# Five buffers in place of three for the samples' raw key pages, in a decoder step on one core

## The chip, the cores and the metric

The kernel runs on one core of one Trainium2 chip. The metric is the device time of one execution in microseconds (us), lower is better. A core has a matrix engine (TensorE, PE in the rows; PEld is its weight load), a vector engine (VectorE, DVE), a scalar engine (ScalarE, ACT), a general engine (GpSimd, POOL) and a queue that issues transfers (SyncE, SP); a q behind an engine's name (SPq, ACTq) is its sequencer. Transfers run on 16 DMA engines.

## The reference, cut to what matters

One step of a two-layer decoder trunk: a gated short convolution, then sparse attention with three branches (compressed, selected, window) that share one set of keys and values. There are 512 prompt tokens and 8 samples of one token each; a sample has 2048 past rows in 16 pages of 128 rows. The part that matters here is the attention of the samples:

```python
def nsa_sample(q, gate, cmp_tok, new_sel, win_all, page_table, pool_sel):
    ...
    def one(q_b, g_b, cmp_b, new_b, win_b, pages):
        def fetch(kp):
            in_past = kp < past_len
            page = pages[jnp.clip(kp // PAGE_SIZE, 0, n_pages - 1)]
            old = pool_sel[page, kp % PAGE_SIZE, :, hidx, :]
            ...
        return nsa_attend(q_b, g_b, pos, cmp_b, fetch, n_blocks, win_b, win_pos)
```

In nsa_attend the scores over the compressed keys give an importance of each block of 64 keys; the 16 most important blocks are attended to, and so are the window's last 512 keys. The kernel does not gather: it scores all 16 pages of every sample and masks the blocks that were not chosen.

## The kernel before, in words

Everything is float32, and the large products are done as three matmuls on split operands (mm3, lines 114 to 116). After the convolution and the query projections the stage that matters begins, at about 740 us of the profiled span. Two streams are written into one another there by mix (line 228):

- The main stream, kvz_steps: the products for the keys and values of the prompt (kv_work, four of them) and for the gate z (z_work, four). It has 68 steps: nine for each kv_work (eight of four matmul triples, and one for the samples' own rows), eight for each z_work (four triples each). Their weights come through a single buffer (wraw, loaded at line 384 from the ACT queue), and are split on ACT and DVE (lines 103, 104).
- The side stream, sample_steps: the samples' attention. RK = 0.8 steps of it are taken for each main step, 54 in all.

The side stream's first part is sample_keys (line 1146). It loads the compressed keys in two halves (kc, line 1191), scores them (line 1180), and works out which blocks are chosen; for that it loads a constant table (lt, line 1215) that DVE reads at line 1221. Then come 40 tiles of raw keys, here called page tiles 1 to 40. Each holds 4 pages (128 rows by 256 numbers each, 512 KB in a tile). Tiles 1 to 32 hold the selected branch's pages and cost SP two register loads of page numbers (line 1356) and four transfers (line 1361); tiles 33 to 40 hold window rows and cost two transfers (line 1370). A page tile is turned by eight transposes on PE (line 1245), copied from PSUM by ACT and DVE into a kt tile (lines 1251, 1249), and each second tile is followed by 16 matmuls for the scores (line 1180). Page tile p belongs to side step 4 + p (for the first 32), so the code's order puts it beside main step (4 + p) / 0.8, rounded up.

kc's two halves, lt, and the 40 page tiles all come from raw_t, in this order, 43 requests in all. raw_t gives a tile of the ring skv, which has three buffers of 4 KB a partition; while the pool pr does not exist (it is made in attention, line 939, after the stage), this is its only source. A new load waits until PE has done the transposes of the tile that had the buffer.

The second part is sample_values (line 1285): softmaxed scores S are transposed into PT (lines 1301 to 1306), a tile of 22 blocks of 128 columns, 11 KB a partition, and the value pages are multiplied by it (line 1320). PT is allocated there, as the last tile of the pool `at`; values are loaded through raw_v, which takes two of three from the kt ring and the third from raw_t.

On SP the stage's instructions keep the order in which the code writes them; on the other engines the order is fixed ahead, by a planner that simulates the program and takes what it believes to be ready. An engine executes its list in order. When the main stream is through, attention loads its constants and the prompt's keys (KK, lines 931 and 1011) into room that the main stream's tiles had, and its first scores are line 1053.

Of the kernel before, what the change touches and what calls it, by code (L numbers as in the profile page):

```python
# [8 lines left out]
F32 = mybir.dt.float32  # L9
# [64 lines left out]
def dram(ap, offset, dims):  # L74
    return bass.AP(tensor=ap.tensor, offset=ap.offset + offset, ap=dims)


class Yoco:
# [10 lines left out]
    at_prompt = None  # L89
    n_raw = 0  # L90
    n_val = 0
    at_w = {}
    pr = None

# [1033 lines left out]
    def sample_setup(self):  # L1128
        self.cst = {}
        self.load_consts(self.at, ("grp", "mem", "mb", "em", "sel"))  # L1130
        self.S = self.at.tile([128, 2704], F32, name="S")

    def raw_t(self):
        self.n_raw += 1
        if self.pr and self.n_raw % (3 + SK) >= 3:
            return self.pr.tile([128, 4, 256], F32, name="skv2", bufs=SK)
        return self.at.tile([128, 4, 256], F32, name="skv", bufs=3)

    def raw_v(self):

        self.n_val += 1
        if self.n_val % 3 == 0:
            return self.raw_t()
        return self.at.tile([128, 2, 512], F32, name="kt", bufs=4).rearrange("p a (b n) -> p (a b) n", b=2)

    def sample_keys(self):

        nc = self.nc
        at = self.at
        I = self.I  # L1150
        cst = self.cst
        S = self.S
        raw_t = self.raw_t
        QF = at.tile([128, 2, 128], F32, name="QF")
        QZ = at.tile([128, 2, NS, 32], F32, name="QZ")
        sm = at.tile([128, 16], F32, name="sm")
# [5 lines left out]
        for kvh in range(4):  # L1162
            hp, h2 = divmod(kvh, 2)
            a = slice(h2 * 64, h2 * 64 + 64)
# [24 lines left out]
        for par in range(2):  # L1189
            kc = raw_t()  # L1190
            nc.sync.dma_start(kc, dram(self.KCd, par * 128 * 256, [[256, 128], [2 * 128 * 256, 4], [1, 256]]))
            scores(acc[:, :128], par, lambda j, hp: kc[:, j, hp * 128:hp * 128 + 128], par == 0, par == 1)
            yield
# [18 lines left out]
        sc = S[:, 256:286]  # L1212
        nc.vector.tensor_copy(sc, ps[:, :30])
        lt = raw_t().rearrange("p a n -> p (a n)")[:, :900].rearrange("p (a n) -> p a n", a=30)
        nc.sync.dma_start(lt, dram(I["consts"], self.lt_at, [[NCONST, 128], [30, 30], [1, 30]]))
        c1 = S[:, 512:1412].rearrange("p (a n) -> p a n", a=30)
# [13 lines left out]
        for br in range(2):  # L1230
            base = 2056 * br
            for c in range(4 if br == 0 else 1):
                d = S[:, base + c * 512:base + (c + 1) * 512]
                acc = self.ps.tile([128, 512], F32, name="acc1", bufs=1)
                for par in range(2):
                    for half in range(2):
                        kt = []
                        for i in range(2):
                            raw = raw_t()
                            pair = at.tile([128, 2, 512], F32, name="kt", bufs=4)  # L1240
                            self.load_keys(raw, br, (4 * i + par, 4 * i + 2 + par), c * 4 + half * 2)
                            for hp in range(2):
                                ps = self.psum1()
                                for x in range(4):
                                    nc.tensor.transpose(ps[:, x * 128:(x + 1) * 128],  # L1245
                                                        raw[:, x, hp * 128:(hp + 1) * 128], self.ident)
                                k = pair[:, hp]
                                if hp:
                                    nc.vector.tensor_copy(k, ps)
                                else:  # L1250
                                    nc.scalar.activation(k, ps, AF.Copy)
                                kt.append(k)
                            if i:
                                scores(acc[:, half * 256:half * 256 + 256], par,
                                       lambda j, hp: kt[j // 2 * 2 + hp][:, j % 2 * 256:j % 2 * 256 + 256],
                                       par == 0 and half == 0, par == 1 and half == 1)
                            yield
# [27 lines left out]
    def sample_values(self):  # L1285

        nc = self.nc
        at = self.at
        cst = self.cst
        S = self.S  # L1290
        raw_t = self.raw_t
        OS = at.tile([128, KT, NS], F32, name="OS")
        PT = at.tile([128, 22, 128], F32, name="PT")
        nc.gpsimd.memset(PT[:, 21], 0.0)

        at_ = [t * 128 for t in range(16)] + [2056 + t * 128 for t in range(4)] + [2576]
        for t in range(0, 21, 4):
            n = min(4, 21 - t)
            ps = self.psum1()
            for i in range(n):  # L1300
                nc.tensor.transpose(ps[:, i * 128:(i + 1) * 128], S[:, at_[t + i]:at_[t + i] + 128], self.ident)
            d = PT[:, t:t + n].rearrange("p t x -> p (t x)")
            if t % 8:
                nc.vector.tensor_copy(d, ps[:, :n * 128])
            else:
                nc.scalar.activation(d, ps[:, :n * 128], AF.Copy)
            yield
        for br in range(2):
            ps = self.psum1()
            a = 2048 + br * 520  # L1310
            nc.tensor.transpose(ps[:NS, :128], S[:, a:a + NS], self.ident)
            nc.vector.tensor_copy(PT[br * 32:br * 32 + NS, 21], ps[:NS, :128])
        yield
        acc = self.ps.tile([128, 512], F32, name="acc1", bufs=1)
        for par in range(2):
            def values(t, rhs, first=None, behind=None):
                for j in (3, 0, 1, 2):
                    q = first or behind
                    with self.tc.issue_after(q.ins) if q else ExitStack():
                        m = nc.tensor.matmul(acc[j * 32:j * 32 + 32, par * 256:par * 256 + 256],  # L1320
                                             PT[:, t, j * 32:j * 32 + 32], rhs(j),
                                             start=par == 0 and t == 20, stop=par == 1 and t == 18)
                    first = first or m
                return first

            vc = raw_t()
            nc.sync.dma_start(vc, dram(self.VCd, par * 128 * 256, [[256, 128], [2 * 128 * 256, 4], [1, 256]]))
            values(20, lambda j: vc[:, j])
            values(21, lambda j: self.VN)
            yield  # L1330

            for t in range(0, 20, 2):
                raw = [self.raw_v(), self.raw_v()]
                for i in range(2):
                    self.load_values(raw[i], t // 16, par, t % 16 + i)

                first = None
                for i in (1, 0):
                    first = values(t + i, lambda j: raw[i][:, j], first, self.at_prompt)
                yield  # L1340
        om = S[:, 0:512]
        nc.vector.tensor_tensor(om, acc, cst["em"], op=ALU.mult)
        nc.vector.tensor_tensor(om[:, 0:256], om[:, 0:256], om[:, 256:512], op=ALU.add)
        ps = self.ps.tile([128, 512], F32, name="acc1", bufs=1)
        for hp in range(2):
            nc.tensor.matmul(ps[:, hp * 32:hp * 32 + 32], om[:, hp * 128:(hp + 1) * 128], cst["sel"],
                             start=True, stop=True)
        nc.vector.tensor_copy(OS.rearrange("p k b -> p (k b)"), ps[:, :64])
        nc.vector.tensor_tensor(OS, OS, self.SZ[:, :, NT:], op=ALU.mult)
        self.split(self.OZS[:, :, 0:NS], self.OZS[:, :, 32:40], OS)  # L1350
        yield
# [165 lines left out]
```

## Time and profile before

| | us |
|---|---|
| runs shown | 1180.73, 1181.22, 1184.16 |
| median | 1181.22 |
| the profiled execution's own time | 1182.27 |
| span of its instructions | 1180.4 |
| PE busy in the span | 1127.1 (95%) |
| DVE, ACT, POOL busy | 686.2, 583.1, 276.1 |

All times of the rows are counted from the span's start. The profiled execution is 1.05 us above the median of the runs, and 1.9 us of it lies outside the span. A stage's limit is read from the idle time of PE inside it and from what ended that idle time.

### The profile page before, as it was taken

What the parts mean: (1) busy time and instruction counts of PE and PEld (TensorE: products, weight loads), DVE (VectorE), ACT (ScalarE), POOL (GpSimd) and SP (SyncE); (2) the same over time, 40 slices, a digit from 0 to 9 for tenths busy, and PEclk for the clock granted to TensorE, in tenths of its full rate; (3) what the DMA queues carried; (4) which work ended last, traced back from release to release, by engine and by line L of the source; (5) the groups of instructions that cost most, each with busy time, mean ns of one, the idle gap of its engine ahead of it and who ended that gap; (6) DMA issues with size and microseconds to landing.
All of it is one profiled execution on the core that took longest, in us unless ns stands there. A gap on an engine that the chain in (4) does not pass through costs nothing.

```text
span 1180.4 us, 23314 instructions
## 1 busy us (share of the span) xinstructions
PE 1127.1 (95%) x8882; PEld 1030.6 (87%) x8882; DVE 686.2 (58%) x1532; ACT 583.1 (49%) x1183; POOL 276.1 (23%) x382
## 2 busy tenths in 40 slices
PE   6999999999999999999999999998999898999896
PEld 4999999999999999999999999877888765766796
DVE  4865464455644555554557466542454698898952
ACT  5454343353343443434446465342445677787651
POOL 5221200201101111012002101120110464565631
PEclk9999999999999999999999999998999899999998
DMA  7564754564446645357532542587986557576011
GB/s 208 154 221 135 252 177 116 188 199 153 135 122 204 199 134 161 119 141 236 162 112 56 134 99 80 157 263 215 244 229 182 204 183 222 170 221 281 2 57 71
DMA packets 161072, 194.81 MB, mean 165 GB/s; under 512 B 48096, under 2 KB 139720, under 8 KB 160312
## 3 DMA queue, kind: packets, MB, share of 16 engines
q1 hardware_dynamic: 122928, 125.32, 35.9%
q0 software_dynamic: 12832, 46.20, 11.6%
q10 hardware_dynamic: 25200, 21.79, 6.4%
q8 instruction: 70, 1.15, 0.4%
q14 instruction: 42, 0.34, 0.1%
HBM read 168.96 MB, written 32.75 MB: 171 GB/s over the span
## 4 chain that ended last, share of the span: by engine, by line
PE 66%; DMA 9%; DVE 9%; issue 8%; ACT 3%; SPq 3%; POOL 3%; POOLq 0%; ACTq 0%; DVEq 0%
PE mm L115 13%; PE mm L116 13%; PE mm L114 13%; PE tr L618 3%; PE acc L116 2%; PE acc L114 2%; PE s L1053 2%; PE acc L115 2%; DMA wrawx<-in_conv_w_in 2%; PE tr L1245 1%; PE acc L1320 1%; PE acc L1115 1%; DVE pp L1060 1%; DMA skv<-in_cache_sel_kv 1%; PE acc L1116 1%
## 5 line engine op out<-in xcount | busy, mean ns | idle before, releaser
L114 PE MATMUL mm<-X,wh 128*128 128x260 f32 (+1 forms) x1008 | 290.3, 288 | 3.2 <-ACT X L355 1.4
L115 PE MATMUL mm<-X,wl 128*128 128x260 f32 (+1 forms) x1008 | 286.1, 284 | 0.1
L116 PE MATMUL mm<-X,wh 128*128 128x260 f32 (+1 forms) x1008 | 285.6, 284 | 0.5 <-DVE X L360 0.5
L114 PEld LDWEIGHTS mm<-X,wh 128*128 128x128 f32 (+1 forms) x1008 | 188.7, 187 | 6.1 <-ACT X L355 1.7
L115 PEld LDWEIGHTS mm<-X,wl 128*128 128x128 f32 (+1 forms) x1008 | 188.8, 187 | 3.5 <-DVE wl L104 0.3
L116 PEld LDWEIGHTS mm<-X,wh 128*128 128x128 f32 (+1 forms) x1008 | 188.6, 187 | 3.7 <-DVE X L360 0.7
L606 POOL DMA_INDIRECT G<-in_cache_cmp_kv,cidx x64 | 62.9, 982 | 329.5 <-ACT Gp L612 163.6
L100 ACT ACTIVATE th<-tr 128x512 fp32r<-128x512 f32 x128 | 71.8, 594 | 96.9 <-PE tr L618 96.5
L101 DVE TENSOR_TENSOR tl<-tr,th 128x512 fp32r<-128x512 f32 x128 | 84.5, 683 | 50.7 <-ACT th L100 50.7
L114 PE MATMUL mm<-X,whx 128*128 128x260 f32 x288 | 81.6, 283 | 0.7 <-ACT whx L100 0.7
L1078 POOL TENSOR_SCALAR pp<-pp,pst,gt 128x128 f32<-128x128 f32 (+3 forms) x128 | 76.6, 612 | 23.9 <-DVE pst L1075 14.9
L115 PE MATMUL mm<-X,wlx 128*128 128x260 f32 x288 | 82.0, 285 | 0.0
L116 PE MATMUL mm<-X,whx 128*128 128x260 f32 x288 | 81.7, 284 | 0.0
L1063 ACT ACTIVATE pp<-pp,pst 128x128 f32<-128x128 f32 (+3 forms) x128 | 70.8, 555 | 13.6 <-DVE pst L1060 12.7
L101 DVE TENSOR_TENSOR wl<-wraw,wh 128x1024 fp32r<-128x1024 f32 x38 | 49.5, 1307 | 40.7 <-ACT wh L100 40.5
L618 PE MATMUL tr<-ident,Gp 128*128 128x128 f32 x512 | 70.7, 272 | 1.2 <-DVE Gp L614 1.2
L100 ACT ACTIVATE wh<-wraw 128x1024 fp32r<-128x1024 f32 x38 | 39.9, 1056 | 54.0 <-PE mm L116 41.0
L618 PEld LDWEIGHTS tr<-ident,Gp 128*128 128x128 f32 x512 | 59.3, 140 | 4.1 <-DVE Gp L614 1.4
L1060 DVE CUSTOM_DVE_ANT_0 pp<-s,c_mw 128x128 f32<-128x128 f32 (+3 forms) x128 | 57.9, 481 | 3.1 <-PE tx L1103 2.2
L114 PEld LDWEIGHTS mm<-X,whx 128*128 128x128 f32 x288 | 54.3, 188 | 2.3 <-ACT whx L100 0.9
L115 PEld LDWEIGHTS mm<-X,wlx 128*128 128x128 f32 x288 | 54.2, 188 | 2.1
L116 PEld LDWEIGHTS mm<-X,whx 128*128 128x128 f32 x288 | 54.4, 189 | 1.3
(434 smaller groups left out, 2849.4 us busy)
## 6 DMA issues: line engine op xcount, KB each, us to landing
skv<-in_cache_sel_kv SPq DMA_DIRECT2D x172, 128.0 KB
wraw<-in_conv_w_in SPq DMA_DIRECT2D x16, 1024.0 KB
wrawx<-in_conv_w_in SPq DMA_DIRECT2D x16, 1024.0 KB
kt<-in_cache_sel_kv SPq DMA_DIRECT2D x84, 128.0 KB
wo<-wo_scratch SPq DMA_DIRECT2D x4, 2048.0 KB
out_win_kv_s<-in_cache_win_kv ACTq DMA_DIRECT2D x8, 1022.0 KB
wrawx<-in_conv_w_out SPq DMA_DIRECT2D x4, 1024.0 KB
wraw<-in_conv_w_out SPq DMA_DIRECT2D x4, 1024.0 KB
```

Of the source, the lines that this page charges most:

```text
L100: nc.scalar.activation(hi, src, AF.Copy)
L101: nc.vector.tensor_tensor(lo, src, hi.bitcast(F32), op=ALU.subtract)
L114: mm(out, sh, mh, start=first, stop=False)
L115: mm(out, sl, mh, start=False, stop=False)
L116: mm(out, sh, ml, start=False, stop=last)
L606: nc.gpsimd.indirect_dma_start(out=G.rearrange("p i c d -> p (i c d)"), out_offset=None, in_=table, in_offset=bass.IndirectOffsetOnAxis(ap ...
L618: nc.tensor.transpose(ps[:, h * 128:(h + 1) * 128], Gp[:, c * 4 + h, :], self.ident)
L1053: nc.tensor.matmul(out, QK[:, g], KK[:, s, cs], start=s == 0, stop=s == 1)
L1060: nc.vector.tensor_tensor_reduce(out=d, in0=src, in1=m, scale=-SCALE, scalar=1e28, op0=ALU.add, op1=ALU.min, accum_out=mx[:, g, i:i + 1])
L1063: nc.scalar.activation(d, d, AF.Exp, scale=-1.0, bias=mx[:, g, i:i + 1], accum_out=l[:, g, i:i + 1])
L1078: nc.gpsimd.tensor_scalar(P[g2][:, i, :W], P[g2][:, i, :W], f[:, g2, i + 1:i + 2], gates[:, g2, i + 1:i + 2], op0=ALU.mult, op1=ALU.mult)
L1115: nc.tensor.matmul(acc, v, ph, start=i == 0, stop=False)
```

## The change: a place of five for the key pages

PT is allocated in sample_setup, behind S, and so lives for the whole stage. sample_keys takes its raw tiles from raw_k in place of raw_t: of each five requests three go to the ring skv as before, and two to fixed places in PT (blocks 0 to 7 and 8 to 15, 4 KB a partition each). sample_values takes the same PT.

```diff
@@ class Yoco
     n_raw = 0
     n_val = 0
+    n_key = 0
@@ sample_setup
         self.S = self.at.tile([128, 2704], F32, name="S")
+        self.PT = self.at.tile([128, 22, 128], F32, name="PT")
@@
+    def raw_k(self):
+
+        self.n_key += 1
+        i = self.n_key % 5
+        if i < 3:
+            return self.raw_t()
+        return self.PT[:, (i - 3) * 8:(i - 2) * 8].rearrange("p t x -> p (t x)").rearrange("p (a n) -> p a n", n=256)
+
@@ sample_keys
-        raw_t = self.raw_t
+        raw_t = self.raw_k
@@ sample_values
-        PT = at.tile([128, 22, 128], F32, name="PT")
+        PT = self.PT
         nc.gpsimd.memset(PT[:, 21], 0.0)
```

Request 1 and 2 (kc) go to the ring, 3 (lt) to PT's first place, 4 (page tile 1) to its second, 5, 6 and 7 (page tiles 2 to 4) to the ring, 8 (page tile 5) to PT's first place, 9 to its second, and so on.

## Rows read from the trace of the kernel before

**Rows 1.** Busy time by stretch (us, each engine's busy time with count, clock, DMA share, GB/s).

```profile
740.00:922.00 182.00, 173.69 (x1574) 152.53 (x1572) 80.78 (x172) 76.81 (x149) 19.47 (x27) 0.98 0.71 206
780.00:800.00 20.00, 15.92 (x147) 12.60 (x149) 8.11 (x15) 7.60 (x15) 6.06 (x7) 1.00 0.84 271
```

**Rows 2.** PE in order of time (start, length), where page tiles 9 to 12 begin.

```profile
787.68 0.51 PE L1245 MATMUL tr<-ident,skv 128*128 128x128 f32 x2 [1.39 <-DMA skv<-in_cache_sel_kv]
...
792.12 0.67 PE L1245 MATMUL tr<-ident,skv 128*128 128x128 f32 x2 [0.28 <-DMA skv<-in_cache_sel_kv]
...
799.11 0.33 PE L1245 MATMUL tr<-ident,skv 128*128 128x128 f32 x1 [2.40 <-DMA skv<-in_cache_sel_kv]
...
802.74 0.48 PE L1245 MATMUL acc<-ident,skv 128*128 128x128 f32 x1 [1.10 <-DMA skv<-in_cache_sel_kv]
```

**Rows 3.** Busy time by stretch, the two stretches around them at the lower clock.

```profile
800.48:807.31 6.83, 5.73 (x27) 5.33 (x28) 1.76 (x4) 2.19 (x5) 0.00 (x0) 0.50 0.74 249
926.78:937.02 10.24, 9.71 (x47) 8.53 (x47) 6.57 (x55) 6.64 (x28) 3.64 (x9) 0.50 1.04 388
```

**Rows 4.** SP's own waits, 744 to 915 us (us in total, times, longest).

```profile
SPq L1361 <- PE tr L1245: 7.8, 4, 3.7
...
SPq L1361 <- PE acc L1180: 3.1, 1, 3.1
...
SPq L1361 <- PE acc L1245: 2.3, 2, 1.8
```

**Rows 5.** Line 1361 from 745 to 883 us (ns min/median/max, first and last start).

```profile
L1361 SPq DMA_DIRECT2D skv<-in_cache_sel_kv x128: 332/333/1178, 749.1 to 881.6; - x128
```

**Rows 6.** SP in order of time: kc, then the first transfer of page tiles 1, 5, 9.

```profile
733.20 0.93 SPq L1191 DMA_DIRECT2D skv<-kc_scratch  x2
...
749.12 0.37 SPq L1361 DMA_DIRECT2D skv<-in_cache_sel_kv  x1
...
764.96 0.33 SPq L1361 DMA_DIRECT2D skv<-in_cache_sel_kv  x1
...
782.50 0.33 SPq L1361 DMA_DIRECT2D skv<-in_cache_sel_kv  x1
```

**Rows 7.** DVE in order of time: the read of lt.

```profile
760.78 1.09 DVE L1221 TENSOR_TENSOR S<-S,skv 128x900 f32<-128x900 f32 x1
```

**Rows 8.** PE in order of time, the end of the main stream and attention's start.

```profile
921.43 0.28 PE L115 MATMUL mm<-X,wl 128*128 128x260 f32 x1
921.55 0.28 PE L116 MATMUL mm<-X,wh 128*128 128x260 f32 x1
...
924.02 0.64 PE L1320 MATMUL acc<-skv,PT 128*32 128x256 f32 x8 [2.08 <-DVE PT L1304]
924.75 0.66 PE L1301 MATMUL tr<-ident,S 128*128 128x128 f32 x4
...
927.33 1.08 PE L1320 MATMUL acc<-VN,PT 128*32 128x256 f32 x8
928.93 6.04 PE L1053 MATMUL s<-KK,QA 128*128 128x160 f32 x24 [0.53 <-DMA KK<-kk_scratch]
```

**Rows 9.** POOL in order of time, the same stretch.

```profile
921.90 0.98 POOL L943 MEMSET pb<- 128x512 f32 x2 [53.61 <-PE mm L116]
922.83 0.73 POOL L1011 DMA_DIRECT2D KK<-kk_scratch  x1
```

**Rows 10.** Line 1301 (ns min/median/max, first and last start, forms).

```profile
L1301 PE MATMUL tr<-ident,S x16: 270/273/330, 916.4 to 925.1; 128*128 128x128 f32 x16
```

**Rows 11.** Line 1282, the same columns.

```profile
L1282 DVE TENSOR_SCALAR S<-S,sm x2: 482/882/1283, 899.5 to 924.2; 128x2056 f32<-128x2056 f32 x1, 128x520 f32<-128x520 f32 x1
```

**Rows 12.** Line 114 by stretch: the main stream's matmuls before page tiles 11 and 32.

```profile
739.60:796.16 56.56, 23.44 (x81) 15.19 (x81) 1.00 0.66 207
739.60:887.08 147.48, 61.00 (x206) 39.49 (x206) 0.98 0.77 222
```

**Rows 13.** The chain of work that ended last, one piece (start, us).

```profile
764.66 7.17 DMA wraw<-in_w_kv
```

## The prediction

> **What bounds the kernel now.** I read the table of times first, then PE's busy time by stretch, then PE in order of time wherever it idles, then SP's own waits, and the end of the stage last. In the stage that the change touches, 740 to 922 us, PE is busy 173.7 of 182 us [rows 1]: PE is the bound, and all that this stage can give is its 8.3 us of idle time and whatever PE runs at half clock. The worst piece is 780 to 800 us, with 4.1 us idle. PE in order of time shows where: four times PE starts the transposes of a page tile and stands until the rest of it has landed, 1.39, 0.28, 2.40 and 1.10 us, released by the transfer of page tiles 9 to 12 [rows 2]. That is 5.17 us. Right behind it the granted clock is 0.50, so 1.2 of 2.4 GHz, from 800.48 to 807.31 us [rows 3]; PE stood until 802.74 [rows 2], so 4.57 us of work ran at half speed, which at full speed takes half: 2.3 us. Stalls and clock make 7.5 us, 0.6% of the run.
>
> Is the ring of three what makes the pages late? Only in part. From 745 to 883 us SP issues 128 page transfers for 32 tiles in 132.5 us, 4.14 us a tile [rows 5], and its waits for PE, which are the waits for a free buffer, add up to 13.2 us [rows 4]: 3.1 for kc's scores and 10.1 for transposes. Without them a tile costs (132.5 - 13.2) / 32 = 3.7 us of SP's own issuing, which no buffer removes. So the ring costs SP a tenth of its pace, and its own issuing nine tenths.
>
> **The change part by part.** *Page tile 1* moves from a kc buffer to PT's second place, which nothing holds. Before, its first transfer went out at 749.12 [rows 6], and 3.1 us of that was the wait for kc's scores [rows 4]; so it goes at about 746, or sooner if SP's order lets it pass the stores before it. *Page tiles 2 to 4* follow through the ring at 3.7 us each.
>
> *Page tile 5* takes PT's first place, where lt was. DVE reads lt from 760.78 for 1.09 us [rows 7], so this load, and everything behind it on SP (page tiles 6 to 40 and the first half of the values), can't go before 761.87. Tiles 1 to 4 take SP until 746 + 4 x 3.7 = 760.8, so the added wait is 1.1 us, or up to 7 if tiles 1 and 2 went out before 740; but either way tile 5 goes at 761.9 in place of 764.96 [rows 6], 3.1 us sooner. This is the pinch: the head start of tiles 1 to 4 is worth no more than that.
>
> *Page tiles 6 to 9* then find their buffers free. SP took 782.50 - 764.96 = 17.5 us from tile 5 to tile 9 [rows 6], with a longest wait of 1.8 us for transposes in it [rows 4]. Without that, tile 9 goes at 761.9 + 15.7 = 777.6: a lead of 4.9 us. PE's lateness behind tiles 9 to 12 adds up to 1.39, 1.67, 4.07 and 5.17 us [rows 2]; if PE asks for them when it did, 4.9 us covers all but 0.3. So the stalls fall by 4.9 us, and the clock, which fell behind them, should hold: 2.3 more. Sum -7.2 us. From below nothing is gained if PE asks as much earlier as the pages come earlier (a rival); from above no more than 7.5 can be had from these tiles.
>
> *Behind tile 12* PE stands for no page in this stage, so a further lead buys nothing there; it moves side work ahead of main work. That has one price. When the main stream ends, at 921.8, POOL clears two tiles and fetches the prompt's keys, and attention's scores start at 928.93 [rows 8, 9]: 7 us which PE fills with what is left of the side stream, 0.64 + 0.66 + 1.08 = 2.4 us of it in these rows [rows 8]. If the side stream is sooner done, this work stands before the main stream's end, and PE idles in its place. Between 0 and 2.4 us, and I take 2.0, since the window tiles wait for transposes too and will move up. The second low stretch of the clock, 926.78 to 937.02 [rows 3], follows this idle time and stays. Sum -7.2 + 2.0 = -5.2 us.
>
> *PT as one tile.* If a wait covered all of PT rather than the part that is touched, tile 1 would wait for lt's reader, 761.9 in place of 749.1, 12.8 us lost at the start. I take nothing: S, one tile too, is read by line 1301 from 916.4 on while line 1282 still writes another part of it at 924.2 [rows 10, 11]. The copies into PT come behind the last transposes through S, so PT's two places are long free. Moving PT ahead shifts the ring and the kt tiles by 11 KB, onto older tiles' room; kc is loaded at 733.20 and lt read 27 us later [rows 6, 7], so a wait of a few us there is covered. In the values the count of raw_t is shifted by the 17 requests that no longer pass it, so that another of its tiles is the one in pr: same buffers, same order, nothing.
>
> Of the bandwidth: the weights of the main stream share the DMA engines, whose share is 0.84 in 780 to 800 us [rows 1], and one of their loads, landing in 7.17 us, is a piece of the chain that ended last [rows 13]. By the Trainium skill (DMA: Bandwidth & Descriptors, section "Issuing engines are not separate DMA queues") transfers from SP and ACT run on the same engines and interleave; by that rule pages sent ahead push the weights back, and the sum goes to nothing (the third rival, which stands on the rows alone).
>
> The profiled execution gives 1182.27 - 5.2 = 1177.1; it lies 1.05 above the median, so 1176.0 for the runs.
>
> **The rivals.**
>
> *The stalls move along.* PE's order is fixed by a planner that sees the same two buffers more. The code's order puts page tile 11 beside main step 19; PE had done 81 of line 114 by then, which is step 22.2 [rows 12], and for tile 32 it is step 55.5 against 45. The side stream runs behind its place, so the planner has room to pull each tile ahead as soon as it believes the page is there; then PE asks as much earlier as SP delivers, and the same 5.2 us of stalls and 2.3 of clock form again. For it: SP's own 3.7 us a tile are nine tenths of its pace. Against it: the pages now arrive ahead of a fixed amount of PE work. Gives 0: 1181.
>
> *Slower: PE is made to ask before SP can deliver.* The same mechanism one step further. A main step is 12 matmuls at 0.12 us from start to start [rows 8], 1.44 us; pulling tiles 9 to 12 from 3.2 steps behind to none asks 4.6 us earlier, against a lead of 4.9: stalls of about 4.9 stay. Pulling tiles 20 to 32 from up to 10.5 steps behind asks up to 15 us earlier against a lead that grows to at most 13.2 [rows 4]: some 3 us of new stalls with a second spell of half clock, 2.3 us, and the work missing at the stage's end, 2.4 us. Sum -0.3 + 3 + 2.3 + 2.4 = +7.4: 1188.6. It decides where the tiles are taken faster than one in 3.7 us over a stretch. Against it: each pull is paid by main work that is still to do, and a planner that leaves tiles 10 steps back before may not pull them all.
>
> *The weights come later.* Two more page tiles in flight are 1 MB; at the 388 GB/s seen at a DMA share of 1.04 [rows 3] that is 2.7 us for a weight load behind them, and there are two in the stretch in question: 5.4 us against the 5.2 gained. Gives 1181 to 1182. Against it: the bytes are the same, so a page sent earlier is out of the way later.
>
> **How the numbers follow.** This kernel's measurement can tell about 0.3%, 3.5 us, from no change. Forecast 0.45: 1176.0, of its own 1173.5 to 1179, nearly all faster. Stalls move along 0.22: 1181, nearly all the same. Asked too early 0.20: 1188.6, nearly all slower. Weights later 0.13: 1181.5, split 0.03, 0.08, 0.02. So faster 0.48, same 0.30, slower 0.22. The range 1170 to 1188 leaves half of the slower case out above, and below it the whole 7.5 us with some luck in a new order of the attention behind it.
>
> **What would show it.** Right: the idle times of PE before line 1245 that a page transfer ended fall from 5.17 to under 1 us; no stretch at 0.50 of the clock between 780 and 860 us; the first transfer of page tile 5 follows the read of lt by a fraction of a us; SP's waits at line 1361 for kc's scores and for transposes fall from 13.2 us to a few, with one wait for DVE new; the main stream's last matmul ends 5 to 7 us sooner, near 915 to 917. Wrong: as many idle us before line 1245, at other tiles (first rival) or more of them behind tile 16 (second); longer waits of line 103 for its weights (third); or attention's first scores that move less than the main stream's end, by more than 2.4 us.

## The result, and the profile after

| | before | changed |
|---|---|---|
| median of 5 runs each, us | 1181.11 (1178.20 to 1184.16) | 1190.95 (1188.41 to 1194.13) |
| ratio, 95% interval | | 1.007 [1.005, 1.0091] |
| the profiled execution's own time | 1182.27 | 1194.13 |
| span of its instructions | 1180.4 | 1192.4 |
| PE busy in the span | 1127.1 | 1133.9 |

The change makes the kernel slower, by 0.5 to 0.9%. The profiled execution of the changed kernel is the slowest of its five; the same kernel run again (five_again, below) was profiled at 1189.02 with a span of 1187.2. The rows of this section are those of the first trace, and what the second has otherwise is said beside them. Ten lines were added above the functions of the stage, so line 1245 is now 1255, 1251 is 1261, 1361 is 1371, 1370 is 1380 and 1221 is 1231; lines 103, 114 and 384 moved by one.

The predicted part came first, and as predicted. SP in order of time, the first transfers of page tiles 1, 5 and 9 (answering to [rows 6]), and its own waits from 744 to 925 us ([rows 4]):

```profile
738.54 0.37 SPq L1371 DMA_DIRECT2D PT<-in_cache_sel_kv  x1
...
763.71 0.33 SPq L1371 DMA_DIRECT2D PT<-in_cache_sel_kv  x1
...
777.39 0.33 SPq L1371 DMA_DIRECT2D skv<-in_cache_sel_kv  x1
```

```profile
SPq L1371 <- DVE S L1231: 4.3, 1, 4.3
SPq L1371 <- PE acc L1255: 2.8, 7, 0.8
SPq L1371 <- PE tr L1255: 2.5, 8, 0.6
```

Tile 9 goes at 777.39 (777.6 was forecast, 782.50 before). SP waits 5.3 us for transposes at line 1371, where it waited 10.1 for them and 3.1 for kc's scores, and the one new wait of size is the pinch at lt, 4.3 us for DVE. In 780 to 800 us PE is now busy 19.65 of 20 us, after 15.92 [rows 1].

Then the time is lost again. Busy time by stretch, as in [rows 1], and the three stretches at half clock with the one at attention's start ([rows 3]):

```profile
740.00:928.30 188.30, 177.37 (x1595) 156.42 (x1594) 83.36 (x181) 79.72 (x154) 20.98 (x29) 0.97 0.69 203
780.00:800.00 20.00, 19.65 (x188) 16.78 (x187) 8.59 (x17) 9.60 (x19) 6.79 (x8) 1.00 0.81 258
...
808.60:812.01 3.41, 3.41 (x19) 3.41 (x17) 0.69 (x1) 1.19 (x2) 0.00 (x0) 0.50 0.61 191
829.08:832.49 3.41, 3.41 (x19) 3.41 (x18) 0.84 (x2) 1.57 (x5) 0.62 (x1) 0.50 0.97 255
866.63:870.04 3.41, 2.87 (x21) 1.63 (x21) 2.20 (x5) 3.41 (x10) 0.44 (x1) 0.50 0.77 257
934.89:948.54 13.65, 11.06 (x50) 9.74 (x54) 8.76 (x67) 9.65 (x35) 6.99 (x16) 0.50 0.85 304
```

PE's waits from 744 to 938 us (us in total, times, longest):

```profile
PE s L1054 <- DMA KK<-kk_scratch: 5.4, 1, 5.4
PE tr L1255 <- ACT kt L1261: 4.7, 2, 3.5
PE acc L1255 <- ACT kt L1261: 3.2, 2, 3.1
PE tr L754 <- DVE kt L1259: 1.6, 1, 1.6
PE tr L1255 <- DMA skv<-in_cache_sel_kv: 0.9, 1, 0.9
```

Pages cost PE 0.9 us where they cost 5.17 [rows 2], and nothing at tiles 9 to 12 (in the second trace no page costs anything, but tile 12 stands 4.26 us behind a copy of ACT). But ACT's copies of the transposed keys, line 1261, which ended no stall of this kind before, cost 7.9 us. PE in order of time, the three largest:

```profile
808.10 0.68 PE L1255 MATMUL tr<-ident,skv 128*128 128x128 f32 x4 [1.23 <-ACT kt L1261]
...
828.80 0.89 PE L1255 MATMUL acc<-ident,skv 128*128 128x128 f32 x4 [3.06 <-ACT kt L1261]
...
867.17 1.12 PE L1255 MATMUL tr<-ident,skv 128*128 128x128 f32 x4 [3.46 <-ACT kt L1261]
```

Each row starts when ACT's copy is done: until then the next transposes find no free PSUM tile. Why is ACT late? Its work is no longer than before (23.5 us for kt in the stage before, 23.4 now). ACT in order of time, at the load of four weight pieces of w_qg, first before, then changed:

```profile
848.77 4.39 ACTq L384 DMA_DIRECT2D wraw<-in_w_qg  x4
```

```profile
852.30 0.42 ACTq L385 DMA_DIRECT2D wraw<-in_w_qg  x1
...
853.06 8.01 ACTq L385 DMA_DIRECT2D wraw<-in_w_qg  x3
...
856.48 0.37 ACTq L385 DMA_DIRECT2D wraw<-in_w_qg  x1
...
860.70 0.37 ACTq L385 DMA_DIRECT2D wraw<-in_w_qg  x1
861.18 0.38 ACT L757 ACTIVATE kvs<-tr 8x256 f32<-8x256 f32 x1 [7.95 <-DMA skv<-in_cache_sel_kv]
```

(The x1 rows at 856.48 and 860.70 are two of the three in the row at 853.06, asked for in a narrow window.) Before, the four pieces went out back to back in 4.39 us. Now the third and fourth take 0.37 us each to issue, but start 3.02 and 3.85 us after ACT was free, and the event that releases each is the landing of a page transfer that SP had issued. Everything behind them on ACT waits too: kvs here, and at 828 us a copy of kt:

```profile
820.57 6.61 ACTq L385 DMA_DIRECT2D wraw<-in_w_qg  x4
...
828.15 0.60 ACT L1261 ACTIVATE kt<-acc 128x512 f32<-128x512 f32 x1 [7.74 <-DMA wraw<-in_w_qg]
```

Summed over the issues of line 384/385 in the stage, ACT stands for the landing of a page transfer 0.13 us before, 13.3 us in the changed kernel and 16.2 us in its repetition. That is the new wait, and the prediction did not have it.

Why must a weight piece wait for a page that has nothing to do with it? The views of the profile don't print it, but the instruction records of the traces hold it. Every transfer tells its landing on a numbered semaphore, a counter that instructions can wait for. The transfers of SP and of ACT use the same eight numbers, where SP issues alone one after the other in a fixed turn, and those of GpSimd use eight others. An issue that takes a number first waits until the transfer that had the number before has landed. In the changed kernel all ten stands of ACT of over 0.15 us that a page transfer ended are of this kind: the number waited for is the one that ACT's transfer then takes itself. So the wait is an instruction of the program; no run shows a limit of the chip behind it. The two page transfers in question, issued by SP at 852.43 and 854.10, landed 4.0 and 6.6 us after their issue; ACT was free for its pieces 1.0 and 2.8 us after it. Before, all 16 pieces of w_qg also took a number from a page transfer, and found it landed 0.02 to 4.4 us earlier.

So it is a race between ACT and the landing, and from the same records the race can be counted over the weight issues from 790 us on. Before, ACT was free a median 4.5 us after the page transfer's issue, and the transfer landed in a median 2.7. In the changed kernel it is 3.9 and 3.9, in its repetition 2.9 and 3.9. More transfers in flight are not the reason: between 745 and 880 us the transfers of SP and ACT under way are 4.2 on average before, 4.1 in the changed kernel and 4.3 in its repetition, and never more than eight.

The trace before had one such stand already, at the store of eight rows (kvs) at 799:

```profile
794.13 0.40 ACTq L384 DMA_DIRECT2D wraw<-in_w_kv  x1
799.14 0.30 ACTq L760 DMA_DIRECT2D out_sel_kv_s<-kvs  x1
```

ACT stood 4.5 us there until a page landed, and it cost PE nothing, since PE itself was standing for page tile 11 from 796.71 to 799.11 [rows 2].

Attention's start costs more as well. PE and POOL at the end of the main stream, answering to [rows 8, 9]:

```profile
927.99 0.28 PE L117 MATMUL mm<-X,wh 128*128 128x260 f32 x1
...
936.68 4.98 PE L1054 MATMUL s<-KK,QA 128*128 128x160 f32 x20 [5.43 <-DMA KK<-kk_scratch]
```

```profile
928.33 0.98 POOL L944 MEMSET pb<- 128x512 f32 x2 [61.26 <-PE mm L117]
```

Main stream to first scores takes 8.4 us in place of 7.1 (7.5 in the second trace), of which PE idles 5.4 (4.5), and the half clock there lasts 13.65 us in place of 10.24 (in both).

### The profile page after: what moved, and what is told of

Read it like the earlier page. It is cut to its first block, busy times and chain, and to the rows that moved or that the text cites. A ratio compares the mean times of both kernels' runs of the same rounds, so it can differ in the third digit from the quotient of the medians.

```text
span 1192.4 us, 23366 instructions
## 1 busy us (share of the span) xinstructions
PE 1133.9 (95%) x8882; PEld 1036.2 (87%) x8882; DVE 689.5 (58%) x1532; ACT 582.0 (49%) x1183; POOL 275.8 (23%) x382
## 4 chain that ended last, share of the span: by engine, by line
PE 70%; DVE 9%; DMA 7%; issue 6%; ACT 4%; POOL 2%; SPq 1%; ACTq 0%; POOLq 0%; DVEq 0%
PE mm L116 13%; PE mm L117 13%; PE mm L115 13%; PE tr L619 3%; PE acc L117 2%; PE acc L115 2%; PE acc L116 2%; PE s L1054 2%; PE acc L1190 2%; PE tr L1255 2%; DMA wrawx<-in_conv_w_in 2%; PE acc L1116 2%; PE acc L1330 2%; PE acc L1117 2%; DVE pp L1061 2%
## 5 line engine op out<-in xcount | busy, mean ns | idle before, releaser
L105 DVE SCALAR_TENSOR_TENSOR wl<-wraw,cols,wh 128x256 fp32r<-128x256 f32 (+1 forms) x96 | 41.5, 485 | 26.5 <-ACT wh L104 21.4
L117 PEld LDWEIGHTS mm<-X,whx 128*128 128x128 f32 x288 | 54.4, 189 | 1.3
```

The source lines that it names most:

```text
L105: nc.vector.scalar_tensor_tensor(lo, src, scale, hi.bitcast(F32), op0=ALU.mult, op1=ALU.subtract)
L117: mm(out, sh, ml, start=False, stop=last)
```

## The experiments

All were timed beside the kernel before on the same chip; the shared medians of before are 1183.41 (first four), 1182.61 (next four), 1183.74 (third four) and 1182.04 (last four). The letters of the theories are not the same in every set: what the second set calls B (page transfers in flight hold up ScalarE's weight transfers) is A in the third and the fourth.

The stretches of every trace, counted alike (us; main stream from its first matmul, at 641 to 646 us, to its last; then to attention's first scores; then to the span's end; and the last piece of that, from the end of the last store's issue). PE's work in the first stretch, its busy time weighted with the granted clock, is 263.5 to 265.9 us in all of them but a_dve (268.6):

| kernel | page buffers | main stream | to scores | to the end | after last store |
|---|---|---|---|---|---|
| before | 3 | 276.3 | 7.1 | 251.5 | 7.3 |
| changed / five_again | 5 | 282.0 / 283.3 | 8.4 / 7.5 | 255.7 / 253.4 | 7.3 |
| pt_early | 3 | 274.2 | 7.7 | 253.4 | 7.4 |
| a_dve / b_dve | 5 / 3 | 280.5 / 279.0 | 7.3 / 7.8 | 248.1 / 245.4 | 7.3 |
| early5 / late5 | 5 then 3 / 3 then 5 | 276.4 / 287.3 | 8.5 / 7.9 | 247.4 / 253.2 | 7.3 |
| a_pool / b_pool | 5 / 3 | 275.5 / 280.6 | 7.2 / 7.4 | 242.8 / 244.8 | 3.2 |
| late5_pool | 3 then 5 | 281.2 | 7.5 | 244.9 | 3.2 |
| a_pool_st / b_pool_st | 5 / 3 | 274.9 / 280.7 | 7.7 / 8.2 | 244.1 / 246.4 | 3.9 / 3.6 |

### Is it the place in memory, or the copies on ACT?

**five_again**: the changed kernel, unaltered.

> The changed kernel once more, for a second profile and its time beside the others. All theories: 1188 to 1194 us. In its profile the two long stands of PE of before's successor (3.06 us at page tile 18, 3.46 us at page tile 27) should come again if they are the program's own: each between 2 and 5 us, ended by ACT's copy into a kt tile. If they are chance of one execution, they are gone or elsewhere.

1189.02 us, ratio 1.0051 [1.0032, 1.007]. The loss repeats. PE's waits in its stage:

```profile
PE tr L1255 <- ACT kt L1261: 7.9, 2, 4.3
PE s L1054 <- DMA KK<-kk_scratch: 4.5, 1, 4.5
PE acc L1255 <- ACT kt L1261: 3.1, 2, 2.7
```

11 us behind ACT's copies, and no wait for a page at all.

**pt_early**: PT allocated early as in the change, the ring of three kept.

```diff
-        raw_t = self.raw_k
+        raw_t = self.raw_t
```

> PT allocated behind S as in the change, but all raw tiles from the ring of three: the move in memory alone. Theories ACT, end of stage, bandwidth: as before, 1179 to 1184. Theory place (new waits on older tiles' room, or a planner's other order from the allocation alone): part or all of the loss, 1185 to 1193.

1181.29 us, ratio 0.999 [0.9976, 1.0004]. PT's early place costs nothing that can be measured, as the prediction had taken it. Against this trace, whose memory is the same, five_again's main stream is 9.1 us longer: 8.0 us more idle time of PE (14.63 against 6.59), and 3.4 us more at half clock, worth 1.7.

**a_dve** and **b_dve**: both copies of the transposed keys on DVE, with five buffers and with three.

```diff
-                                if hp:
-                                    nc.vector.tensor_copy(k, ps)
-                                else:
-                                    nc.scalar.activation(k, ps, AF.Copy)
+                                nc.vector.tensor_copy(k, ps)
```

> Five buffers, and both copies of each page tile into kt are on DVE (before: one of two on ACT). Theory ACT: PE stands because a PSUM bank waits for ACT's copy, and ACT stands in its list behind transfers of weights, which wait for semaphores that page transfers have; with the copies off ACT these stands (6.5 us) and the spells of half clock behind them (about 3 us) go: 1178 to 1184. Theory end of stage: the loss is that side work is done too early and that attention begins at half clock; the copies change nothing of that: 1188 to 1194. Theory bandwidth: weights land later, PE's main matmuls wait for them: 1187 or more.

> Three buffers, and both copies of each page tile into kt on DVE: the control for the same edit without the change. Theory ACT: before, PE hardly stood for ACT's copies in this stage, so nothing: 1178 to 1184. If DVE (80 of 182 us busy in the stage, and 40 copies of 0.69 us more) becomes late itself: 1184 to 1190.

a_dve 1182.59, ratio 0.9994 [0.9976, 1.0013]; b_dve 1178.54, ratio 0.996 [0.994, 0.998]. Both are where theory ACT put them: without copies on ACT the kernel with five buffers is 6.4 us faster than five_again. ACT stands no shorter than in five_again at its weight transfers (21.0 us in a_dve, 2.9 in b_dve), but PE stands for it only 0.3 us. What PE waits for in a_dve is spread:

```profile
PE tr L1255 <- DMA skv<-in_cache_sel_kv: 2.7, 3, 1.3
PE tr L1255 <- DVE kt L1258: 2.5, 2, 2.3
PE acc L1255 <- DMA PT<-in_cache_sel_kv: 1.8, 2, 1.6
```

But three buffers are still 4 us better than five here (by the stretches 1.5 in the main stream and 2.7 behind the first scores), so this pair alone can't tell whether the stands on ACT are all of it.

### Which page tiles lose, and is it that PE asks earlier?

**early5** and **late5**: five buffers up to page tile 12 and three behind it, and the reverse.

```diff
-        if i < 3:
+        if i < 3 or self.n_key > 15:      # early5;  late5: <= 15
```

> Five buffers up to page tile 12, a ring of three from tile 13 on (the places in the later P tensor are used by the compressed keys, lt and page tiles only until then). TensorE's written order is that of the five-buffer kernel from tile 13 on up to tile 32 (tile 20 after 80 first-product matmuls of the main stream since tile 1, before 92; tile 30 after 141, before 153). Theory A (the loss comes from TensorE asking for page tiles earlier than ScalarE, the transfers and the waits can serve them): the gain at tiles 9 to 12 is there, and from tile 13 TensorE stands for pages that three buffers bring late, so no gain is left: 1183 to 1189 us where the kernel before has 1183.4. Theory B (it comes from the five buffers themselves: more page transfers in flight, whose landings ScalarE's weight transfers wait for): with three buffers behind tile 12 these waits are as before, and the predicted gain is seen alone: 1177 to 1180.

> The reverse: a ring of three up to page tile 12, five buffers from tile 13 on. The written order of TensorE is as before up to tile 17 and then still earlier than in the five-buffer kernel (tile 40 after 172 first products, five buffers throughout 185, before 204). Theory A: no gain at tiles 9 to 12, and the side work runs out sooner, so more of the wait for KK is bare: 1190 to 1194. Theory B: the loss of the late part without the gain of the early one: five buffers cost 5.6, and 5 of gain is taken away, 1192 to 1195. The two differ little here; what is looked for is whether early5 and late5 together make up the five-buffer kernel's difference.

early5 1179.90, ratio 0.9984 [0.9963, 1.0005]; late5 1191.89, ratio 1.0071 [1.0049, 1.0092]. The two differences, -2.7 and +9.3, add up to 6.6, near the 5.6 to 9.8 of the whole change (late5 lies in theory A's range and 0.1 us under theory B's): a small gain in front of tile 13, and a loss behind it. Theory A of this set expected no gain in early5, and the sign went against it, though the interval touches 1. early5's ACT does stand 12.5 us at weight transfers, 9.8 of it behind 845 us, where the ring of three is back: theory B gave the right time, but the waits are not as before. They cost PE 4.8 us, less than in late5 (7.1, with 6.1 us for pages besides). PE's waits in late5:

```profile
PE acc L1190 <- ACT kt L1261: 5.7, 1, 5.7
PE acc L1255 <- DMA skv<-in_cache_sel_kv: 4.3, 3, 1.8
PE tr L1255 <- DMA skv<-in_cache_sel_kv: 1.8, 2, 1.3
...
PE acc L1255 <- ACT kt L1261: 1.4, 2, 1.1
```

**a_rk07** and **b_rk07**: 0.7 side steps for each main step, with five buffers and with three.

```diff
-RK = 0.8
+RK = 0.7
```

> Five buffers, and the rate of side work to main steps 0.7 in place of 0.8: TensorE's written order then has tile 20 after 104 first products and tile 40 after 204, which is where the kernel before has its last ones (92 and 204). Theory A: with the order no earlier than before, the five buffers keep their gain and lose nothing; against the three-buffer kernel at the same rate (b_rk07) it is faster by 2 to 6 us. Theory B: against b_rk07 it is slower by 3 to 6 us as at rate 0.8.

> The control: the kernel before with the rate 0.7. More side work is left for the wait for KK and for the attention, and fewer page tiles are asked for at the pinch behind lt. Both theories: within 4 us of the kernel before (1180 to 1187); it only serves a_rk07.

a_rk07 1201.71, ratio 1.0165 [1.014, 1.019]; b_rk07 1197.41, ratio 1.0134 [1.0108, 1.016]. b_rk07 misses its range by 10 us: the side work that the lower rate leaves over goes into the attention, where the stretch to the end is 267.8 us in b_rk07 against 251.5 before. The difference of the pair, 4.3 us to the disadvantage of five buffers, has the sign that theory B of this set asked for, but the two intervals overlap; this pair settles nothing.

### Taking ACT's transfers away

**a_pool** and **b_pool**: the stage's weight pieces issued by GpSimd, with five buffers and with three. **late5_pool**: the same edit in late5.

```diff
-            (nc.sync if self.wide else nc.scalar).dma_start(r3[:, :, off:off + w], src)
+            (nc.sync if self.wide else nc.gpsimd).dma_start(r3[:, :, off:off + w], src)
```

> Five buffers, and the main stream's raw weights (3 pieces of w_kv and 16 of w_qg in the stage) issued by GpSimd in place of ScalarE, so that no instruction of ScalarE stands behind a transfer that waits for page transfers in flight. Theory A (ScalarE's copies of the transposed keys stand behind those transfers: stalls of 1.2 to 3.5 us at TensorE in the stage, 10.6 us in the repeated run): these stalls go, and the time falls by 5 to 8 us against the five-buffer kernel, to 1181 to 1184, and lies within 2 us of its control with three buffers (b_pool). Theory B (five buffers pull page tiles ahead and the work is missing elsewhere, or the pages' own transfers take the memory): ScalarE free of the transfers changes only who is late; still 4 to 7 us above b_pool.

> The control: three buffers, raw weights issued by GpSimd. ScalarE's waits at the weights in the kernel before are some 17 us, of which TensorE feels 1.3 us; both theories: 1179 to 1184.

> Three buffers up to page tile 12, five from tile 13 on (the arrangement that cost most, 9.3 us above the kernel before), with the raw weights issued by GpSimd. Theory A: the cost behind tile 12 goes with the transfers from ScalarE: within 2 us of b_pool. Theory B: at least 5 us above b_pool.

a_pool 1171.92, ratio 0.9914 [0.9893, 0.9936]; b_pool 1177.78, ratio 0.996 [0.9941, 0.998]; late5_pool 1178.10, ratio 0.9959 [0.9941, 0.9976]. This is the decisive set, and a_pool misses its forecast on the good side: theory A expected 1181 to 1184 and no more than 2 us from b_pool. (b_pool lies 1.2 us under its own range, late5_pool where theory A put it.) With ACT's queue clear of the weights, five buffers are 5.9 us faster than three (0.9914 / 0.996 = 0.9954, and with both intervals taken as independent about 0.9925 to 0.9983), 5.1 us of it in the main stream's stretch. Five buffers behind tile 12 alone, which cost 9.3 us with the weights on ACT, cost 0.3 us here and gain nothing.

That 5.9 lies near the 5.2 which was forecast for the change is in part luck, since the traces don't show the gain where the prediction put it. PE's waits for pages, first b_pool, then a_pool_st, a kernel with five buffers that is described below:

```profile
PE tr L1245 <- DMA skv<-in_cache_sel_kv: 8.5, 7, 3.4
...
PE tr L1245 <- DMA skv<-in_cache_win_kv: 0.7, 1, 0.7
```

```profile
PE tr L1255 <- DMA skv<-in_cache_sel_kv: 2.8, 2, 2.1
PE acc L1255 <- DMA skv<-in_cache_sel_kv: 2.0, 1, 2.0
```

In b_pool 6.0 us of the 9.2 are at tiles 9 to 11. In a_pool no page costs anything, but a stall of 6.66 us at tile 12, behind ACT (see below), takes the place of those 6.0, and what is gone is the 3.0 us behind tile 12. In the pair a_pool_st and b_pool_st it is the other way round: PE idles 5.3 us less up to tile 12, and 2.2 us more behind it. So the pairs show what five buffers are worth, 5.9 and 7.4 us, and not that all of it is gained in front of tile 13.

GpSimd's issues of the weights wait for DVE to free the buffer, as they must, and for no page:

```profile
L385 POOL DMA_DIRECT2D wraw<-in_w_qg x16: 884/892/912, 820.1 to 881.5; - x16
...
  DVE wl L105: 41.4, 6
  issue: 1.4, 1
```

And the written order of PE in a_pool is nearly as early as in the changed kernel: 84, 150 and 184 matmuls of line 115 stand between page tile 1 and tiles 20, 32 and 40 (changed: 86, 141, 185; before: 92, 166, 204). Being asked earlier does not by itself make the kernel slow.

Both pool kernels also end sooner for another reason, which has to be kept out of the comparison with before. The last store's issue, before and in a_pool, whose spans are 1180.4 and 1169.2 us:

```profile
1172.84 0.34 ACTq L1476 DMA_DIRECT2D out_y_p<-y  x1
```

```profile
1165.68 0.34 ACTq L1486 DMA_DIRECT2D out_y_p<-y  x1
```

The span goes on for 7.3 us behind it before, and for 3.2 us in a_pool and b_pool. The difference is an instruction that closes GpSimd's list; the longest of the three DRAINs is the one meant (ns min/median/max), before and in a_pool:

```profile
L1513 POOLq DRAIN  x3: 46/99/8110, 1171.5 to 1180.2; - x3
```

```profile
L1523 POOLq DRAIN  x3: 46/99/2313, 1164.4 to 1168.9; - x3
```

The long one ends 0.8 us ahead of the span's end before; in a_pool it is through 2.5 us ahead of it, and the last stores' landing comes later. So 4.1 us of the pool kernels' gain on before is this end, and only the pair tells what the buffers do.

**early5_dve**: early5 with both copies on DVE.

> A version meant to beat both: five buffers up to page tile 12, three from 13 on, and both copies of the transposed keys on VectorE. If the gain at tiles 9 to 12 (2.7 us in early5) and that of the copies on VectorE with three buffers (4.9 us) add up: 1174 to 1176. If both remove the same stalls: as with the copies alone, 1178 to 1179.

1180.52, ratio 0.9976 [0.9958, 0.9994]. This is above both ranges. The gains don't add up; it is no better than b_dve. Here PE waits 4.6 us for pages in the stage, and the attention takes 253.2 us, against 247.4 in early5.

### What is left: small stores

In a_pool one large stall remained. ACT in order of time, and PE behind it:

```profile
791.93 0.63 ACT L109 ACTIVATE st<-kvt 128x512 fp32r<-128x512 f32 x1 [1.05 <-DMA kk_scratch<-st]
802.19 0.30 ACTq L761 DMA_DIRECT2D out_sel_kv_s<-kvs  x1
802.54 0.60 ACT L1261 ACTIVATE kt<-tr 128x512 f32<-128x512 f32 x1 [9.97 <-DMA skv<-in_cache_sel_kv]
...
803.19 1.11 PE L1255 MATMUL tr<-ident,skv 128*128 128x128 f32 x4 [6.66 <-ACT kt L1261]
```

A store of eight rows stands for 9.6 us until a page transfer has landed whose number it takes, and PE pays 6.66 us. It is the store that stood 4.5 us before, and 7.5 us in b_pool, without a cost to PE. **a_pool_st**, **b_pool_st** and **a_st** move the stage's stores of kvt and kvs to GpSimd: beside the weights with five buffers, with three, and alone with five. **a_pool_2** is a_pool again on their chip.

```diff
-                nc.scalar.dma_start(dram(op, (t * 128 * 2 + c) * 256, [[512, 128], [1, 256]]), kvt)
+                nc.gpsimd.dma_start(dram(op, (t * 128 * 2 + c) * 256, [[512, 128], [1, 256]]), kvt)
```

(and the same for the two stores of kvs)

> Five buffers; raw weights and the stage's stores of kvt and kvs issued by GpSimd, so ScalarE issues no transfer at all between the pages. Theory A (any transfer of ScalarE waits for page transfers in flight, whatever its size): the 6.66 us stall of a_pool goes, and with it 3 to 6 us: 1166 to 1169. Theory C (the cost lay in the weights alone, the long store wait was chance): within 2 us of a_pool.

> The control with three buffers. TensorE stands 9.2 us for pages in b_pool and not at all for ScalarE's copies. Theory A and C: within 2 us of b_pool (1176 to 1180).

> Five buffers; only the stores moved, the raw weights still on ScalarE. Theory A: the stalls at ScalarE's copies in the five-buffer kernel stand behind weight transfers (four waits of 2.3 to 3.9 us after 823), so little goes: 0 to 3 us below the five-buffer kernel, 1185 to 1189. Theory C: the same.

> a_pool again, beside the three others: 1171 to 1174; it serves them as reference.

a_pool_st 1172.08, ratio 0.9924 [0.9909, 0.9938]; a_pool_2 1173.27, ratio 0.9934 [0.9916, 0.9952], inside its range; b_pool_st 1179.51, ratio 0.9979 [0.996, 0.9997], inside its range; a_st 1182.07, ratio 1.0 [0.9986, 1.0014]. The stall behind ACT's copies goes entirely, as A said, but the time does not follow: PE now stands for pages where it stood for the copy. The two rows of a_pool_st above are these waits, 4.8 us at tiles 13 and 27.

So C's number came out, by another road than C's. The mechanism does hold for small stores; their price in this kernel is hidden by the next wait. With five buffers against three the difference is 7.4 us here. a_st lies 3 us under its range; its end behind the last store is 3.3 us, so 4 us of that is the shorter end, and with it taken out (1186) it is where it was expected, with 9.1 us of stalls behind ACT's copies still there.

a_pool and a_pool_st are the best versions that were run, 0.5 to 1.1% faster than before.

## Why the prediction was wrong

The sum was -7.2 + 2.0 = -5.2, with nothing for ACT. The main stream's last matmul, forecast for 915 to 917, came at 928.27.

- *Tiles 1 to 9 on SP.* Right in kind, with the pinch at lt: the new wait was 4.3 us, inside the 1.1 to 7 given. That tile 9 came nearly to the number (777.39 against 777.6) is luck: tile 1 went out at 738.54 and not 746, tile 5 at 763.71 and not 761.9, since lt was read later, and SP then took 13.7 us to tile 9 and not 15.7. The page stalls at tiles 9 to 12 went as forecast, 5.17 to 0.
- *The clock.* The spell behind tiles 9 to 12 went, but three others came, behind ACT's stalls (the first also behind the 0.91 us for a page): that no stretch at 0.50 would come between 780 and 860 failed twice.
- *The wait for KK.* Priced at 2.0. PE's idle time there went from 0.5 us at the scores and 2.1 us at a value tile [rows 8] to 5.4 us (4.5 in the second trace), 2 to 3 us more, and the longer half clock at attention's start adds up to 1.7 us. Right in kind and somewhat small.
- *PT as one tile, the shift of memory.* Taken at nothing, and pt_early measured nothing.
- *The step that failed* is "Behind tile 12 PE stands for no page in this stage, so a further lead buys nothing there; it moves side work ahead of main work. That has one price." The medians of late5_pool and b_pool, 0.3 us apart, bear out the first half. The second is wrong: the lead has a second price, at ACT. Its issues come closer behind the page transfers whose semaphore numbers they take (a median 2.9 to 3.9 us after them, 4.5 before), and ACT then stands until those have landed. The prediction looked at what PE waits for and at SP's queue, and took ACT's 16 weight issues as free since they cost 0.13 us of waiting before. What covered them was that ACT came late enough, by as little as 0.02 us. Three buffers alone don't keep that cover, as early5 shows. In the changed kernel ACT stands 13 to 16 us in the stage, and PE pays 7.9 to 11 us of it, and the clock behind. Measured as a whole: the change is +5.6 to +9.8 us with the weights on ACT and -5.9 us with them on GpSimd, so the missing term is some 12 to 16 us, an estimate that takes the two differences as if nothing else changed between them.
- *The rivals.* The slower one, 1188.6, was nearest in size and had PE's order right (tiles 32 and 40 pulled ahead by 25 and 19 matmuls of line 115), but for the wrong reason: the new stalls were not pages that SP could not deliver, and a_pool with nearly the same early order is fast. The stalls did not move along. The third rival had the right parties, weights against pages, and the wrong place: it made weights land later, while the loss is in the wait ahead of their issue and falls on a bystander, ACT's copies. Its premise of two more page tiles in flight did not come true either, with 4.1 to 4.3 transfers under way on average after 4.2.

Of the rule weighed there, in the Trainium skill (DMA: Bandwidth & Descriptors, "Issuing engines are not separate DMA queues"): it adds that starting transfers from several engines saves only the issuing sequencer's time, which it calls usually small. The rows agree on the issue itself, 0.37 us in those above, and moving it to GpSimd saved none of that (0.89 us each); what counted here is the wait ahead of the issue, 13.3 us, of which the sentence does not speak. Why the standing doesn't show as a long row fits the same skill's Perfetto Trace Analysis ("DMA Instruction — HWDGE (DVE, Sync)"): a transfer's reported start is the moment when all its semaphores are satisfied. The rows at 856.48 and 860.70 agree, 0.37 us long with the wait in the gap ahead of them.

**What stays open.** No kernel was run that keeps the weights on ACT and gives them numbers of their own, which would test the shared numbers by themselves; a_pool changes the engine and the numbers at once. Why ACT comes closer behind the page transfers with five buffers, and why these take longer to land, was not followed; the order that the planner wrote and SP's own pace may both be in it. In a_dve and b_dve five buffers are 4 us slower with ACT's copies out of the way; that part was not traced further. And every edit changes the order that the planner writes, so single differences of 2 to 3 us, above all in the attention (242.8 to 255.7 us), are not taken as shown.

## What to carry to other kernels

A buffer more moves the order in which engines issue, also of engines that never touch the buffer: before adding one, look at every engine that issues transfers and computes in the same list, ask which transfers share its semaphores, and price a stand at its issue, not only the transfer's time. A wait of 0.1 us in the profile is no evidence that an issue is free; ask by how much it came late enough. If an engine's copies hold PSUM, let another engine issue its transfers, one that has nothing urgent behind them and does not share the numbers. And when a stall is taken away, look at what stood in its shadow: the small store's 4.5 us cost nothing until the pages were on time.

## What the hardware showed beside that

- In these programs a transfer issued by ACT waited up to 10.3 us (a_pool_2; 9.6 in a_pool) for the landing of an unrelated one issued by SP, even a store of eight rows, because both use one semaphore in turn. Transfers issued by GpSimd, on eight other numbers, waited for no page in any of the seven kernels where it took over weights or stores, at 0.89 us an issue (median in a_pool) against 0.43 for the same weights on ACT in the changed kernel.
- Every kernel with the stage's weights, its stores or both on GpSimd ended 3.2 to 3.9 us after the issue of its last store; all eleven others took 7.3 to 7.4 us. GpSimd's closing DRAIN took 8.1 us in those eleven, where GpSimd issues 91 transfers, and 2.0 to 2.5 us in the seven, where it issues 111 to 141. What makes it shorter was not looked for.
